# Odd layer's output product: two of four column chunks as a Strassen pair, streamed with the first chunk

## The chip, the cores and the metric

The kernel runs on one core of a Trainium2 chip. The metric is device time in microseconds of one execution. Before the change it is 1306.67 us, the median of three runs (1305.98 to 1306.85).

## The reference, cut to what matters

Two post-LayerNorm layers work on `x` of 256 tokens by 2048 channels, in fp32. The even layer is a Mamba-2 mixer beside block attention, with one output projection. The odd layer, where most of the change lies, is:

```python
u, gate = jnp.split(x @ w_in, 2, axis=-1)
y = jax.nn.gelu(s5_ssm(u, ...))
ga, gb = jnp.split(y @ w_glu, 2, axis=-1)
y = ga * jax.nn.sigmoid(gb)
h = (y * jax.nn.silu(gate)) @ w_out           # the odd layer's output product, 2048 x 2048
x = layer_norm(DEEPNORM_ALPHA * x + h, ln_g[layer], ln_b[layer])
```

## The kernel before, in words

**Weights.** Every weight matrix is read once from HBM, in units of 128 partitions by 1024 fp32 values (two K tiles of 128 rows by 512 output columns, 512 KB). A unit goes through three steps, all issued by `split_to` (L328): a load into a `raw` tile (four of them) on SyncE's queue (L361), a rounded copy `wh` on ScalarE (L367), and the remainder `wl = raw - wh` on VectorE (L372). The pool has four `wh`/`wl` pairs, and a unit is split three units ahead of its use. A product of activations and weights takes three matmuls per tile: high by high, high by low, low by high. `xmm` (L417) issues them with the activations as the stationary side: 128 tokens by 128 K rows against 512 columns. So a whole unit is 12 matmuls (two K tiles, two token halves, three terms).

**Strassen groups.** For the odd layer's GLU product, three pairs of column chunks (n1, n2) already use the scheme that the change extends (`product_fast`, L496, with the stream `STREAM`). Over eight of the 16 K tiles, seven products of quarter blocks take the place of eight. A unit of such a product is 6 matmuls (one token half). The names are: p1, q5, v2 and p4 use the weight block `a` (first as loaded, then after `b`, then `c`, then `d` were added to it in place), p3 and q7 use `c` (then `c + b`), and p2 uses `d`. n1 and n2 are the other eight K tiles, done in the plain way. A block is an SBUF tile `block`; "load" is a plain DMA, "add" a DMA issued by GpSimd that adds HBM data onto the block (L324), and "sum" an add on VectorE (L326). An add onto a block follows the split that read the block, and the next split of the block follows the add.

**Order around the change.** SyncE's queue carries the unit loads, in order; GpSimd's queue carries the adds, in order, and each of its DMAs waits in that queue for what it needs. Small work (residual adds, gates, transposes) is put into `jobs` and handed out by `pump` after each unit. A scheduler then fixes each engine's order.

**Output product before.** Four column chunks (j = 0 to 3) of eight units each follow one another: `first2` at L1855, j = 1 and 2 in the loop above `last`, each followed by a residual add and `bn_stats` (`res1`), and j = 3 in `product_apart` (L587), which does all eight units for the first token half and then for the second, so that LayerNorm of the first half runs beside the second. The eight split units of j = 3 are kept in a pool of their own (`tp2`).

**Rotary jobs.** In the even layer `rope_jobs` (L1126) queues two `rot` jobs, two empty ones and two `turn` jobs. `rot` ends with an add on GpSimd (L1143), and `turn` is four TensorE transposes (L626) of what it wrote.

Of the kernel before, what the change touches and what calls it, by code (L numbers as in the profile page):

```python
# [16 lines left out]
P = 128  # L17
# [20 lines left out]
def _stream():  # L38
    out, seen = [], {}
    for g in range(GROUPS):  # L40
        for s in FLOW if g else HEAD:
# [148 lines left out]
def trunk(tc, io, out):  # L190
# [4 lines left out]
    def nm(s):  # L195
        count[0] += 1
        return f"{s}_{count[0]}"

    with ExitStack() as top:
# [76 lines left out]
        for g in range(GROUPS):  # L276
            for k in range(2):
# [50 lines left out]
        def split_to(i):  # L328
            while nsplit[0] <= min(i, len(units) - 1):
                n = nsplit[0]  # L330
                for what in first.get(n, ()):
                    prepare(*what)
                if n in early:
                    with tc.issue_after(loaded[-1].ins):
                        early.pop(n)()
                if n in held_raw:
                    raw = blocks[held_raw[n]]
                elif n in room:
                    raw = keep[0].tile([P, UK, 512], F32R, tag=room[n], name=nm("raw")).bitcast(F32)
                else:  # L340
                    raw = st.tile([P, UK, 512], F32, tag="raw", name=nm("raw"))
                if n < 2:
                    wh = st.tile([P, UK, 512], F32R, tag="wh", name=nm("wh"))
                    wl = st.tile([P, UK, 512], F32R, tag="wl", name=nm("wl"))
                    for k in range(UK):
                        if k == 0:
                            xpart(n)
                        for lo, hi in ((0, 256), (256, 512)) if n + k == 0 else ((0, 512),):
                            loaded.append(nc.sync.dma_start(raw[:, k, lo:hi], units[n][:, k * 512 + lo : k * 512 + hi]))
                            with tc.issue_after(conv[-2].ins):  # L350
                                conv.append(A.activation(wh[:, k, lo:hi], raw[:, k, lo:hi], AF.Copy))
# [11 lines left out]
                wh = pool.tile([P, UK, 512], F32R, tag=th, name=nm("wh"))  # L363
# [4 lines left out]
                wl = pool.tile([P, UK, 512], F32R, tag=tl, name=nm("wl"))  # L368
                with ExitStack() as pin:
                    if hold[0] is not None:  # L370
                        pin.enter_context(tc.issue_after(hold[0]))
                    splits[n] = (loaded[-1], high, V.tensor_tensor(wl, raw, wh.bitcast(F32), op=OP.subtract))  # L372
                ready[n] = (wh, wl)
                for what in then.get(n, ()):
                    prepare(*what)
                nsplit[0] += 1
# [116 lines left out]
                    run(lambda o=o: total(o))  # L493
                then(h)

        def product_fast(stream, group, rest, turn):  # L496
# [6 lines left out]
            for i, (g, s, k) in enumerate(stream):  # L503
                if g not in made:
                    made[g] = group(g, lambda i, names=names: main.tile([P, 512], F32, tag=names[i], name=nm("main")))
                    names = [names[2], names[3], names[1], names[0]]
                split_to(unit[0] + 3)
                wh, wl = ready.pop(unit[0])
                ps, pieces, done = made[g][s]
                if s in ("n1", "n2"):  # L510
                    for j in range(UK):
                        for o in range(2):
                            xmm(ps, o, (wh, wl), j, rest(UK * k + j), s == "n2" and k + j == 0 and (o == 1 or (g, "z") not in open_), False, True)
# [138 lines left out]
        with ExitStack() as l0:  # L652
# [473 lines left out]
            def rope_jobs(ps, dst):  # L1126
# [378 lines left out]

        ax.close()

        with ExitStack() as l1:
# [174 lines left out]
            def scanned():  # L1683
                scan.close()
                gpool.append(l1.enter_context(tc.tile_pool(name="gp", bufs=1)))
                for n in ("n1", "n2", "n4"):
                    ops[n] = gpool[-1].tile([P, 2, 4, P], F32R, name=n)

            at(36, scanned)
            sg1 = wk.tile([P, 2, D], F32, tag="sg1", bufs=1, name="sg1")  # L1690
# [129 lines left out]
            def group(g, bank):  # L1820
# [20 lines left out]
                def one():  # L1841
# [5 lines left out]
                return {"p1": (X, lambda: whole(range(0, 4), 0), [copy("p1", "p1", X)]), "q5": (Y, lambda: summed("n1"), [copy("z5", "gt", Y)]),  # L1847
                        "v2": (X, lambda: summed("n2"), [less(0)]), "q7": (X, lambda: summed("s3"), [less(1)]),
                        "p3": (Z, lambda: summed("n4"), []), "p2": (Y, lambda: whole(range(4, 8), 0), []),
                        "p4": (X, lambda: whole(range(4, 8), 1), []), "n1": ((Y, X), None, []), "n2": ((Z, R), None, []),  # L1850
                        "second": (last2, second), "one": one}

            product_pair(y5hl, between, glu_jobs, lambda: y_split(3))
            product_fast(STREAM, group, lambda k: y5hl(8 + k), 1)
            first2 = product("x", y2hl)  # L1855

        with ExitStack() as l2:
            tp = l2.enter_context(tc.tile_pool(name="tp2", bufs=1))
            keep[0], keep[1] = tp, range(unit[0] + 2 * CU, unit[0] + 3 * CU)
            gb1 = big("A", [P, 4, D])  # L1860
            endp = l2.enter_context(tc.tile_pool(name="endp", bufs=1, space=PSUM))
            sums = [endp.tile([P, 512], F32, name=f"sum{i}") for i in range(2)]
            flip = endp.tile([2, P], F32, name="flip")
            gbr = tp.tile([2, 2 * NEND], F32, name="gbr")
            pair = tp.tile([P, 2], F32, name="pair")
            rowp = tp.tile([2, P], F32, name="rowp")
# [5 lines left out]
            def res1(ps, j, t):  # L1872
                dst = x1[:, t, 512 * j : 512 * j + 512]
                V.scalar_tensor_tensor(dst, dst, ALPHA, ps[t], op0=OP.mult, op1=OP.add)
                V.bn_stats(st1[:, t, j, :], dst)
# [78 lines left out]
```

## Time and profile before

| | before |
|---|---|
| median of three runs | 1306.67 us |
| the profiled execution | 1306.54 us |
| its span (first to last instruction) | 1304.8 us |
| TensorE matmul busy | 1296.0 us (99%) |
| VectorE / ScalarE / GpSimd busy | 1031.8 / 738.1 / 349.2 us |
| DMA moved | 300.90 MB, mean 231 GB/s |

The profile is of one execution. It gives each instruction's start and length, the idle time of the engine before it and what ended that idle time; the chain of waits follows the end of the program back from step to step. Matmuls overlap in the pipeline: one is shown as 0.39 us long, while the next starts 0.23 us after it. The queue that carries GpSimd's DMAs is called q0 software_dynamic, SyncE's is in q1 hardware_dynamic.

### The profile page before, as it was taken

The page shows a single profiled execution, that of the slowest core. Times are in us where ns is not written, and L with a number is a line of the kernel's source. Part 1 is how long each engine was busy: PE and PEld are TensorE (multiplying, and loading weights), DVE is VectorE, ACT ScalarE, POOL GpSimd, SP SyncE. Part 2 cuts the span into 40 slices and gives each one's busy share as a digit, 9 for nine tenths or more (in the row PEclk, how much of TensorE's full clock was granted, in tenths as well). Part 3 has the DMA queues.
Part 4 walks back from the last instruction along what each step waited for, and adds up shares of the span by engine and source line. Part 5 has one row for each costly group of instructions (what it writes and reads, how often), then busy time and mean ns, then how long its engine had stood idle before and what let it go on. Part 6 is the DMA issues. An engine that isn't in the chain of part 4 may idle for free.

```text
span 1304.8 us, 21605 instructions
## 1 busy us (share of the span) xinstructions
PE 1296.0 (99%) x7939; PEld 1089.7 (84%) x7939; DVE 1031.8 (79%) x1694; ACT 738.1 (57%) x1000; POOL 349.2 (27%) x649
## 2 busy tenths in 40 slices
PE   9999999999999999999999999999999999999997
PEld 9988888878888888888888888888888888888885
DVE  6778977885788888888877777858989859988665
ACT  6566668865644554464475555354355557666441
POOL 0044000125035767876820110022232001110000
PEclk9999999999999999999999999999999999999999
DMA  8555566565557766767768978469999789888762
GB/s 316 177 179 188 180 209 198 190 204 178 182 197 244 233 224 228 239 210 245 235 207 291 302 186 291 170 219 324 317 292 327 245 311 241 217 249 230 257 212 80
DMA packets 100094, 300.90 MB, mean 231 GB/s; under 512 B 19378, under 2 KB 29570, under 8 KB 99476
## 3 DMA queue, kind: packets, MB, share of 16 engines
q1 hardware_dynamic: 74356, 239.81, 55.0%
q0 software_dynamic: 11232, 46.18, 13.5%
q10 hardware_dynamic: 14400, 13.54, 3.2%
q8 instruction: 62, 1.02, 0.3%
q14 instruction: 44, 0.36, 0.1%
HBM read 276.93 MB, written 21.00 MB: 228 GB/s over the span
## 4 chain that ended last, share of the span: by engine, by line
PE 95%; POOL 2%; DVE 1%; DMA 1%; issue 0%; ACT 0%; SPq 0%; POOLq 0%
PE main L422 51%; PE main L478 17%; PE main L479 9%; PE main L521 7%; PE main L445 3%; PE aux L626 2%; POOL c L906 1%; PE aux L1084 1%; PE enc L1593 1%; PE dec L1638 1%; PE aux L982 1%; PE aux L1170 0%; DMA wb<-c 0%; POOL c L909 0%; DMA raw<-in_wi 0%; PE dec L1634 0%
## 5 line engine op out<-in xcount | busy, mean ns | idle before, releaser
L372 DVE TENSOR_TENSOR wl<-raw,wh 128x1024 fp32r<-128x1024 f32 x400 | 497.0, 1247 | 194.6 <-ACT wh L367 191.8
L367 ACT ACTIVATE wh<-raw 128x1024 fp32r<-128x1024 f32 x400 | 421.9, 1059 | 403.1 <-PE main L422 184.0
L422 PE MATMUL main<-wh,A 128*128 128x512 f32 x1216 | 392.5, 394 | 0.0
L478 PE MATMUL main<-A,wh 128*128 128x512 f32 x768 | 273.3, 400 | 0.0
L422 PEld LDWEIGHTS main<-wh,A 128*128 128x128 f32 x1216 | 227.9, 188 | 47.3 <-issue 0.7
L422 PE MATMUL main<-wh,C 128*128 128x512 f32 x832 | 265.1, 393 | 0.0
L422 PE MATMUL main<-wl,A 128*128 128x512 f32 x608 | 238.5, 392 | 0.0
L479 PE MATMUL main<-A,wl 128*128 128x256 f32 x768 | 215.5, 281 | 0.0
L422 PEld LDWEIGHTS main<-wh,C 128*128 128x128 f32 x832 | 155.9, 188 | 33.2
L478 PEld LDWEIGHTS main<-A,wh 128*128 128x128 f32 x768 | 144.2, 188 | 35.0 <-ACT b L1057 0.4
L422 PE MATMUL main<-wl,C 128*128 128x512 f32 x416 | 162.6, 391 | 0.0
L479 PEld LDWEIGHTS main<-A,wl 128*128 128x128 f32 x768 | 145.0, 189 | 0.4 <-issue 0.2
L422 PEld LDWEIGHTS main<-wl,A 128*128 128x128 f32 x608 | 114.3, 188 | 22.8 <-issue 0.2
L906 POOL TENSOR_TENSOR c<-c 128x8 f32<-128x8 f32 (+2 forms) x192 | 102.1, 550 | 27.8 <-DMA wb<-c 20.1
L422 PEld LDWEIGHTS main<-wl,C 128*128 128x128 f32 x416 | 78.1, 188 | 16.0
L372 DVE TENSOR_TENSOR wl<-block,wh 128x1024 fp32r<-128x1024 f32 x60 | 72.9, 1221 | 15.1 <-ACT wh L367 14.9
L367 ACT ACTIVATE wh<-block 128x1024 fp32r<-128x1024 f32 x60 | 63.1, 1060 | 36.5 <-PE main L422 20.1
L478 PE MATMUL main<-C,wh 128*128 128x512 f32 x192 | 68.3, 400 | 0.0
L1092 POOL TENSOR_TENSOR ssq<-ssq,c 128x256 f32<-128x256 f32 x16 | 18.0, 1128 | 161.1 <-ACT c L1090 160.4
L479 PE MATMUL main<-C,wl 128*128 128x256 f32 x192 | 53.5, 281 | 0.0
L908 POOL TENSOR_TENSOR c<-c,c 128x4 f32<-128x4 f32 (+2 forms) x96 | 42.2, 440 | 7.5
L324 POOL DMA_DIRECT2D block<-in_wglu x18 | 15.5, 916 | 104.0 <-DVE wl L372 86.7
(367 smaller groups left out, 1731.2 us busy)
## 6 DMA issues: line engine op xcount, KB each, us to landing
raw<-in_wi SPq DMA_DIRECT2D x270, 512.0 KB
raw<-in_wo SPq DMA_DIRECT2D x84, 512.0 KB
raw<-in_wglu SPq DMA_DIRECT2D x46, 512.0 KB
wt<-wb POOLq DMA_DIRECT2D x16, 896.0 KB, 8.3
block<-in_wglu POOLq DMA_DIRECT2D x20, 512.0 KB, 8.1
wb<-ob ACTq DMA_DIRECT2D x16, 512.0 KB
block<-in_wo POOLq DMA_DIRECT2D x12, 512.0 KB, 7.5
block<-in_wglu SPq DMA_DIRECT2D x12, 512.0 KB
```

Source lines behind the costliest of these rows:

```text
L324: added.append(nc.gpsimd.dma_start(blocks[g, name, k].rearrange("p k n -> p (k n)"), source[by][k], accum_op=OP.add))
L367: high = A.activation(wh, raw, AF.Copy)
L372: splits[n] = (loaded[-1], high, V.tensor_tensor(wl, raw, wh.bitcast(F32), op=OP.subtract))
L422: end = T.matmul(ps[o], l[:, k, sl], r[:, j, :], start=start and i == 0, stop=stop and i == 2, skip_group_check=free)
L445: T.matmul(pv[o // 2][:, o % 2, :], l[:, j, sl], r[:, k, :], start=first and i == 0 and o % 2 == 0, stop=end and i == 2 and o % 2 == 1, sk ...
L478: T.matmul(ps[o], wh[:, j, sl], xx[:, k, :, :].rearrange("p a n -> p (a n)"), start=first, stop=False, skip_group_check=True)
L479: lastmm[:] = [T.matmul(ps[o][:, S : 2 * S], wl[:, j, sl], xh[:, k, :], start=False, stop=end, skip_group_check=True)]
L521: lastmm[:] = [T.matmul(ps, p, q[:, j, :], start=begin, stop=False, skip_group_check=True)]
L626: end = T.transpose(dst[:, i * P : i * P + P], s, ident)
L906: G.tensor_tensor(p[:, :, :, 0:m], cs[:, :, :, 1 : m + 1], cs[:, i, :, n : n + 1].unsqueeze(1).to_broadcast([P, 2, 4, m]), op=OP.mult)
L908: G.tensor_tensor(cs[:, 0, :, n + 1 : n + 1 + m], p0[:, 0, :, 0:m], p1[:, 1, :, 0:m], op=OP.subtract)
L1092: G.tensor_tensor(ssq, ssq, jk[:, f, :], op=OP.add)
```

## The change

The first three column chunks of the output product become one stream (`LSTREAM`, handed to `product_fast`): chunk n0 plain, with its eight units, and chunks n1 and n2 as a Strassen pair over K tiles 0 to 7 (p and q names) and plain over tiles 8 to 15. That is 30 units, 16 of 12 matmuls and 14 of 6, in place of 24 units of 12. All weight sums of this pair are DMA adds. The left operands are sums of quarter blocks of `y2`, the product's input, kept as a high and a low part: `rows_job` copies two quarter pairs of the high part into two `block` tiles and adds the low part, all by GpSimd's DMAs; `pair_job` makes four sums of them on VectorE; `again` splits each into high and low on ScalarE and VectorE. These jobs are queued inside the last GLU group (`ahead`). The last chunk keeps four of its split units in the big tile `A`, the other four stay in the ordinary pool, and `LEAP` splits further ahead over the last six units of the stream. The pools of the end are replaced by tiles that exist already (`sg1`, `ut`, `gt` and two PSUM tiles), and the LayerNorm rows are loaded into `sg1`'s place. Rotary jobs get a third empty job.

```diff
+LAST = ("n0 n0 n0 p1 n0 p1 n0 n0 n0 n0 q5 q5 p3 n2 p3 n2 v2 v2 n2 n2 q7 q7 p2 n1 p2 n1 p4 p4 n1 n1").split()
+LSTREAM = [("f", s, LAST[:i].count(s)) for i, s in enumerate(LAST)]
+LEAP = [0] * (len(LAST) - 6) + [1, 1, 2, 2, 3, 4]
...
-        units += [io["wo1"][i] for i in range(io["wo1"].shape[0])]
+        n0, n1, n2, n3 = ([io["wo1"][CU * c + u] for u in range(CU)] for c in range(4))
+        sources["f"] = {"a": n1[0:2], "b": n2[0:2], "c": n2[2:4], "d": n1[2:4], "n0": n0, "n1": n1[4:], "n2": n2[4:]}
...
+        for k in range(2):
+            hook(first, "f", k, "p1", k - 4, "load", "a", "a")
+            hook(first, "f", k, "p1", 1 + k, "load", "c", "c")
+            at_item(then, "f", k, ("p1", k), "add", "a", "b")
+            at_item(then, "f", k, ("q5", k), "add", "a", "c")
+            at_item(then, "f", k, ("p3", k), "add", "c", "b")
+            at_item(then, "f", k, ("v2", k), "add", "a", "d")
+        units += n3
...
-                split_to(unit[0] + 3)
+                split_to(unit[0] + 3 + (leap[i] if leap else 0))
...
-                jobs.extend([rot(0), rot(1), rest, rest, turn(0), turn(1)])
+                jobs.extend([rot(0), rot(1), rest, rest, rest, turn(0), turn(1)])
...
-                return {"p1": (X, lambda: whole(range(0, 4), 0), [copy("p1", "p1", X)]), "q5": (Y, lambda: summed("n1"), [copy("z5", "gt", Y)]),
-                        "v2": (X, lambda: summed("n2"), [less(0)]), "q7": (X, lambda: summed("s3"), [less(1)]),
+                ahead = g == GROUPS - 1
+                return {"p1": (X, lambda: whole(range(0, 4), 0), [copy("p1", "p1", X)]),
+                        "q5": (Y, lambda: summed("n1"), [copy("z5", "gt", Y)] + [rows_job] * ahead),
+                        "v2": (X, lambda: summed("n2"), [less(0)] + [lambda: jobs.extend([pair_job(p) for p in FIRST])] * ahead),
+                        "q7": (X, lambda: summed("s3"), [less(1)] + [lambda: jobs.extend([again(p) for p in ("n1", "n2", "n4", "s3")])] * ahead),
...
+            def rows_job():
+                for i in range(2):
+                    whole2[i] = gpool[-1].tile([P, UK, 512], F32, tag="block", bufs=8, name=nm("block")).rearrange("p k (f n) -> p (k f) n", n=S)
+                for i in range(2):
+                    nc.gpsimd.dma_start(whole2[i], y2["h"][:, 4 * i : 4 * i + 4, :].bitcast(F32))
+                for i in range(2):
+                    nc.gpsimd.dma_start(whole2[i], y2["l"][:, 4 * i : 4 * i + 4, :].bitcast(F32), accum_op=OP.add)
...
             product_fast(STREAM, group, lambda k: y5hl(8 + k), 1)
-            first2 = product("x", y2hl)
...
+            keep[0], keep[1] = keeper, range(unit[0] + len(LAST), unit[0] + len(LAST) + 4)
+            product_fast(LSTREAM, outer1, lambda i: y2hl(8 + i), 0, LEAP)
...
-            for j in range(3):
-                ps = product("x", y2hl, prelude=lambda u: split_to(unit[0] + 3 + u) if j == 2 else None) if j else first2
-                for t in range(2):
-                    jobs.append(lambda ps=ps, j=j, t=t: res1(ps, j, t))
```

`outer1` (new) is the stream's counterpart of `group`: p1, v2, q7 and p4 accumulate in one PSUM bank, q5 and p2 in a second, p3 with n2 and n1 in further ones, and VectorE adds or subtracts each into the residual `x1`, 9 passes over 128 by 512 for chunks n1 and n2 where there were 4.

How the change moves instructions on GpSimd's queue, in the last two GLU groups: the blocks 11667 and 11681 belong to the group before the last, 12015 and 12029 are the last group's `a`, 12117 and 12133 its `c`. Before:

```order
L324 DMA block_11667<-in_wglu 128x1024 [waits DMASW7_49,DMASW3_49,DVE_49]
L324 DMA block_11681<-in_wglu 128x1024 [waits DMASW4_49,DMASW0_49,DVE_49]
L324 DMA block_12015<-in_wglu 128x1024 [waits DMAHW1_49,DMASW5_49,DVE_49]
L324 DMA block_12029<-in_wglu 128x1024 [waits DMAHW3_49,DMASW6_49,DVE_49]
L324 DMA block_12117<-in_wglu 128x1024 [waits DMAHW5_49,DVE_49]
L324 DMA block_12133<-in_wglu 128x1024 [waits DMAHW7_49,DVE_49]
```

and after (12238 and 12239 are the two tiles of `rows_job`, `C_11454` is `y2`):

```order
L343 DMA block_11667<-in_wglu 128x1024 [waits DMASW7_49,DMASW3_49,DVE_49]
L343 DMA block_11681<-in_wglu 128x1024 [waits DMASW4_49,DMASW0_49,DVE_49]
L1885 DMA block_12238<-C_11454 128x4x256 [waits DMASW5_49,DMASW1_49,DVE_49]
L1885 DMA block_12239<-C_11454 128x4x256 [waits DMASW6_49,DMASW2_49,DVE_49]
L1887 DMA block_12238<-C_11454 128x4x256 [waits DMASW5_49]
L1887 DMA block_12239<-C_11454 128x4x256 [waits DMASW6_49]
L343 DMA block_12015<-in_wglu 128x1024 [waits DMAHW1_49,DVE_49]
L343 DMA block_12029<-in_wglu 128x1024 [waits DMAHW3_49,DVE_49]
L343 DMA block_12117<-in_wglu 128x1024 [waits DMAHW5_49,DMASW3_49,DVE_49]
L343 DMA block_12133<-in_wglu 128x1024 [waits DMAHW7_49,DMASW4_49,DVE_49]
```

The four DMAs of `rows_job` stand ahead of the last group's first adds, and the second two of them wait in the queue for the first two to land.

On TensorE in the even layer, at one of the rotary turns (`b_549` and `b_556` are what the two `rot` jobs wrote). Before:

```order
L422 MATMUL main_3867<-wh_3903,A_73 128x512
L626 MATMUL aux_4048<-consts,b_549_3886 128x128 x4
L422 MATMUL main_3866<-wh_3961,A_73 128x512
L422 MATMUL main_3866<-wl_3963,A_73 128x512
...
L422 MATMUL main_3867<-wh_3961,A_73 128x512
L626 MATMUL aux_4084<-consts,b_556_3919 128x128 x4
```

and after:

```order
L442 MATMUL main_3867<-wh_3903,A_73 128x512
L442 MATMUL main_3866<-wh_3961,A_73 128x512
L442 MATMUL main_3866<-wl_3963,A_73 128x512
...
L442 MATMUL main_3867<-wl_3963,A_73 128x512
L442 MATMUL main_3867<-wh_3961,A_73 128x512
L646 MATMUL aux_4078<-consts,b_549_3886 128x128 x4
```

The turn stands one unit of 12 matmuls later.

## Rows read from the trace of the kernel before

**Rows 1.** The profile page: its first line.
```profile
span 1304.8 us, 21605 instructions
```

**Rows 2.** Chain of waits from 1130 us: start us, us, what.
```profile
1159.28 2.77 PE main L521 x12
1162.05 5.44 PE main L422 x24
1167.49 2.72 PE main L521 x12
...
1170.44 1.36 PE main L521 x6
1171.80 2.49 PE main L422 x11
...
1215.59 79.11 PE main L422 x346
```

**Rows 3.** Timeline of TensorE, 512 to 522 us: start, length, instruction, idle before.
```profile
517.88 0.66 PE L626 MATMUL aux<-consts,b 128*128 128x128 f32 x4 [0.96 <-POOL b L1143]
```

**Rows 4.** Busy time by stretch: PE, PEld, DVE, ACT, POOL, clock, DMA share, GB/s.
```profile
1164.00:1172.00 8.00, 8.00 (x37) 6.64 (x36) 7.84 (x10) 5.54 (x9) 0.86 (x1) 1.00 0.43 105
1181.00:1206.00 25.00, 25.00 (x114) 20.69 (x113) 20.51 (x22) 15.41 (x18) 0.00 (x0) 1.00 0.74 227
1206.50:1294.70 88.20, 88.20 (x390) 72.47 (x389) 53.41 (x61) 35.69 (x38) 3.78 (x4) 1.00 0.57 192
```

**Rows 5.** Timeline of GpSimd, 1133 to 1156 us: the adds onto blocks.
```profile
1133.61 0.86 POOL L324 DMA_DIRECT2D block<-in_wglu  x1 [2.08 <-DVE wl L372]
1135.18 0.86 POOL L324 DMA_DIRECT2D block<-in_wglu  x1 [0.71 <-DVE wl L372]
1153.25 0.86 POOL L324 DMA_DIRECT2D block<-in_wglu  x1 [17.20 <-DMA raw<-in_wglu]
1154.98 0.86 POOL L324 DMA_DIRECT2D block<-in_wglu  x1 [0.87 <-DVE wl L372]
```

**Rows 6.** DMA view, one stretch per add of Rows 5: us to landing at the end.
```profile
block<-in_wglu POOLq DMA_DIRECT2D x1, 512.0 KB, 10.3
...
block<-in_wglu POOLq DMA_DIRECT2D x1, 512.0 KB, 12.5
...
block<-in_wglu POOLq DMA_DIRECT2D x1, 512.0 KB, 5.4
...
block<-in_wglu POOLq DMA_DIRECT2D x1, 512.0 KB, 6.4
```

**Rows 7.** DMA queues, 1148.5-1153 and 1156-1159 us: packets, MB, engines' share.
```profile
q1 hardware_dynamic: 517, 1.87, 102.1%
...
q0 software_dynamic: 158, 0.58, 103.7%
```

**Rows 8.** Timeline of SyncE: first and last of six loads issued from 1136.8 us.
```profile
1136.88 0.45 SPq L319 DMA_DIRECT2D block<-in_wglu  x1
...
1150.64 0.33 SPq L361 DMA_DIRECT2D raw<-in_wglu  x1
```

**Rows 9.** Timelines of VectorE and ScalarE in the same stretch.
```profile
1141.55 1.23 DVE L372 TENSOR_TENSOR wl<-block,wh 128x1024 fp32r<-128x1024 f32 x1
...
1162.03 2.38 DVE L372 TENSOR_TENSOR wl<-block,wh 128x1024 fp32r<-128x1024 f32 x2
...
1167.13 1.22 DVE L372 TENSOR_TENSOR wl<-block,wh 128x1024 fp32r<-128x1024 f32 x1
...
1160.94 2.21 ACT L367 ACTIVATE wh<-block 128x1024 fp32r<-128x1024 f32 x2 [0.41 <-PE main L521]
```

**Rows 10.** VectorE by line, 1206.5 to 1294.7 us: count, busy, mean ns, idle before.
```profile
L372 DVE TENSOR_TENSOR wl<-raw,wh 128x1024 fp32r<-128x1024 f32 x29 | 35.3, 1224 | 24.7 <-ACT wh L367 24.7
L1874 DVE SCALAR_TENSOR_TENSOR D<-D,main 128x512 f32<-128x512 f32 x7 | 4.8, 680 | 5.1 <-PE main L422 5.1
```

More of the change, by code (lines that the diff above doesn't have):

```diff
@@ L290, in trunk @@
                 hook(then, g, k, "v2", k, "add", "a", "d")
-        units += [io["wo1"][i] for i in range(io["wo1"].shape[0])]
+        n0, n1, n2, n3 = ([io["wo1"][CU * c + u] for u in range(CU)] for c in range(4))
+        sources["f"] = {"a": n1[0:2], "b": n2[0:2], "c": n2[2:4], "d": n1[2:4], "n0": n0, "n1": n1[4:], "n2": n2[4:]}
+        for g, s, k in LSTREAM:
+            place[g, s, k] = len(units)
+            if s in ("n0", "n1", "n2", "p2"):
+                units.append(sources[g]["d" if s == "p2" else s][k])
+            else:
+                held_raw[len(units)] = (g, "c" if s in ("q7", "p3") else "a", k)
+                units.append(None)
+        for k in range(2):
[6 more added lines that the diff above has]
+        units += n3
         ready = {}
@@ L362, in split_to @@
                 pool, th, tl = (keep[0], f"wh{n % 8}", f"wl{n % 8}") if n in keep[1] else (st, "wh", "wl")
-                wh = pool.tile([P, UK, 512], F32R, tag=th, name=nm("wh"))
+                own = n in keep[1] and callable(keep[0])
+                wh = keep[0](n, 0) if own else pool.tile([P, UK, 512], F32R, tag=th, name=nm("wh"))
                 with ExitStack() as pin:
@@ L367, in split_to @@
                     high = A.activation(wh, raw, AF.Copy)
-                wl = pool.tile([P, UK, 512], F32R, tag=tl, name=nm("wl"))
+                wl = keep[0](n, 1) if own else pool.tile([P, UK, 512], F32R, tag=tl, name=nm("wl"))
                 with ExitStack() as pin:
@@ L494, in product_wide, with product_fast @@
                 then(h)
-        def product_fast(stream, group, rest, turn):
+        def product_fast(stream, group, rest, turn, leap=None):
             names = [f"m{(turnno[0] - turn + i // 2) % 2}{i % 2}" for i in range(4)]
@@ L506, in product_fast @@
                     names = [names[2], names[3], names[1], names[0]]
-                split_to(unit[0] + 3)
+                split_to(unit[0] + 3 + (leap[i] if leap else 0))
                 wh, wl = ready.pop(unit[0])
-                ps, pieces, done = made[g][s]
-                if s in ("n1", "n2"):
+                ps, pieces, done = made[g][s]() if callable(made[g][s]) else made[g][s]
+                if s in ("n0", "n1", "n2"):
                     for j in range(UK):
                         for o in range(2):
-                            xmm(ps, o, (wh, wl), j, rest(UK * k + j), s == "n2" and k + j == 0 and (o == 1 or (g, "z") not in open_), False, True)
+                            xmm(ps, o, (wh, wl), j, (pieces or rest)(UK * k + j), k + j == 0 and (s == "n0" or s == "n2" and (o == 1 or (g, "z") not in open_)), False, True)
                     if s == "n2":
@@ L1506, in trunk @@
         ax.close()
-        with ExitStack() as l1:
+        l1 = enter(ExitStack())
+        if True:
             wk = l1.enter_context(tc.tile_pool(name="wk1", bufs=2))
@@ L1686, in scanned @@
                 for n in ("n1", "n2", "n4"):
-                    ops[n] = gpool[-1].tile([P, 2, 4, P], F32R, name=n)
+                    ops[n] = gpool[-1].tile([P, 2, 4, P], F32R, tag=n, bufs=1, name=nm(n))
             at(36, scanned)
@@ L1851, in group @@
                         "second": (last2, second), "one": one}
+            FIRST = (("n1", (0, 1), (1, 1), OP.subtract), ("n2", "n1", (0, 0), OP.subtract),
+                     ("n4", "n2", (1, 0), OP.add), ("s3", (0, 0), (0, 1), OP.subtract))
+            whole2, sums2, ops2 = {}, {}, {}
+            def rows_job():
[5 more added lines that the diff above has]
+                    nc.gpsimd.dma_start(whole2[i], y2["l"][:, 4 * i : 4 * i + 4, :].bitcast(F32), accum_op=OP.add)
@@ new lines, in pair_job, with go, again @@
+            def pair_job(what):
+                def go():
+                    name, x, y, op = what
+                    i = len(sums2)
+                    sums2[name] = sg1[:, i // 2, 512 + 512 * (i % 2) : 1024 + 512 * (i % 2)].rearrange("p (f n) -> p f n", f=4)
+                    x, y = (sums2[v] if isinstance(v, str) else whole2[v[0]][:, :, v[1] * P : v[1] * P + P] for v in (x, y))
+                    V.tensor_tensor(sums2[name], x, y, op=op)
+                return go
+            def again(name):
+                def go():
+                    if name == "s3":
+                        t = w1("ut", [P, 2, 4, P], 1, F32R)
+                    else:
+                        t = gpool[-1].tile([P, 2, 4, P], F32R, tag=name, bufs=1, name=nm(name))
+                    ops2[name] = t
+                    A.activation(t[:, 0], sums2[name], AF.Copy)
+                    V.tensor_tensor(t[:, 1], sums2[name], t[:, 0].bitcast(F32), op=OP.subtract)
+                return go
@@ L1853, in trunk, with part1 @@
             product_pair(y5hl, between, glu_jobs, lambda: y_split(3))
             product_fast(STREAM, group, lambda k: y5hl(8 + k), 1)
-            first2 = product("x", y2hl)
[L1857 to L1866, printed above, removed]
+            def part1(j, t):
+                return x1[:, t, 512 * j : 512 * j + 512]
@@ new lines, in stat1, with more1, scale1, res1 @@
+            def stat1(j, t):
+                V.bn_stats(st1[:, t, j, :], part1(j, t))
+            def more1(j, t, ps):
+                return lambda: V.tensor_tensor(part1(j, t), part1(j, t), ps, op=OP.add)
+            def scale1(j, t, ps):
+                return lambda: V.scalar_tensor_tensor(part1(j, t), part1(j, t), ALPHA, ps, op0=OP.mult, op1=OP.add)
+            def res1(ps, j, t):
+                scale1(j, t, ps[t])()
+                stat1(j, t)
+            def outer1(g, bank):
+                X, Y = bank(0), bank(1)
+                ps0 = [bank(2), bank(3)]
+                zr = []
+                def ZR():
+                    if not zr:
+                        zr.extend([bank(2), bank(3)])
+                    return zr
+                def less1(t):
+                    return lambda: V.tensor_tensor(part1(2, t), part1(2, t), X, op=OP.subtract)
+                def piece(k, t):
+                    return lambda: [(y2["h"][:, i, t * P : t * P + P], y2["l"][:, i, t * P : t * P + P]) for i in range(4 * k, 4 * k + 4)]
+                def summed2(name):
+                    return lambda: [(ops2[name][:, 0, i, :], ops2[name][:, 1, i, :]) for i in range(4)]
+                def second():
+                    for t, ps in enumerate(ZR()):
+                        jobs.extend([more1(2, t, ps), lambda t=t: stat1(2, t)])
+                def one():
+                    more1(1, 0, Y)()
+                    scale1(1, 1, X)()
+                    jobs.extend([lambda t=t: stat1(1, t) for t in range(2)])
+                return {"n0": (ps0, y2hl, [lambda: jobs.extend([lambda t=t: res1(ps0, 0, t) for t in range(2)])]),
+                        "p1": (X, piece(0, 0), [scale1(1, 0, X)]), "q5": (Y, summed2("n1"), [scale1(2, t, Y) for t in range(2)]),
+                        "v2": (X, summed2("n2"), [less1(0)]), "q7": (X, summed2("s3"), [less1(1)]),
+                        "p3": lambda: (ZR()[0], summed2("n4"), []), "p2": (Y, piece(1, 0), []), "p4": (X, piece(1, 1), []),
+                        "n1": ((Y, X), None, []), "n2": lambda: (ZR(), None, []), "second": (last_of(LSTREAM, g), second), "one": one}
@@ new lines, in trunk, with keeper @@
+            half = big("A", [P, 4, D], F32R)
+            def keeper(n, low):
+                i = n - keep[1].start
+                return half[:, i, 1024 * low : 1024 * low + 1024].rearrange("p (k n) -> p k n", k=UK)
+            keep[0], keep[1] = keeper, range(unit[0] + len(LAST), unit[0] + len(LAST) + 4)
+            product_fast(LSTREAM, outer1, lambda i: y2hl(8 + i), 0, LEAP)
+            gb1 = wk.tile([P, 2, D], F32, tag="sg1", bufs=1, name="gb1")
+            both = sp.tile([P, 2, 512], F32, tag="enc", name=nm("sums"))
@@ L1867, in trunk @@
+            sums = [both[:, i, :] for i in range(2)]
+            flip = sp.tile([P, 2, 512], F32, tag="dec", name=nm("flip"))[0:2, 0, 0:P]
+            gbr = w1("ut", [P, 4, S], 1).rearrange("p a b -> p (a b)")[0:2, 0 : 2 * NEND]
+            small = w1("gt", [P, 2, 256])
+            pair, rowp = small[:, 0, 0:2], small[0:2, 1, 0:P]
             nc.sync.dma_start(gbr, io["lnr"][2:4, 0 : 2 * NEND])
@@ L1870, in trunk @@
             nc.gpsimd.dma_start(gb1[:, 1, :], lnrow(3))
[L1872 to L1875, printed above, removed]
-            for j in range(3):
-                ps = product("x", y2hl, prelude=lambda u: split_to(unit[0] + 3 + u) if j == 2 else None) if j else first2
-                for t in range(2):
-                    jobs.append(lambda ps=ps, j=j, t=t: res1(ps, j, t))
             def last(ps):
```

## The prediction

> **What bounds the kernel now.** I read the busy shares first, then the chain of waits, the lines, the waits of single engines, and the DMA view. TensorE is busy 1296.0 us of the 1304.8 us span [rows 1], and the last product alone is one unbroken piece of the chain, 346 matmuls in 79.11 us [rows 2]. That is 79.11 / 346 = 0.2286 us from one matmul to the next. So here a matmul left out is time saved, if the next one is ready; every unit that comes late is time lost. What must be read is therefore: how many matmuls go, and whether the weight splits (ScalarE, VectorE) and the adds onto blocks (GpSimd's queue) still come in time.
>
> **Matmuls.** Before, the output product has 4 x 8 units of 12 matmuls, 384. After, the stream has 16 units of 12 and 14 of 6, 276, and the last chunk 96: 372. Twelve fewer at 0.2286 us are -2.74 us. This is small because the Strassen pair covers half of the K tiles and saves one product of eight over them.
>
> **Rotary turn.** One TensorE instruction of the even layer waits 0.96 us for the add on GpSimd [rows 3]. With the turn one unit (12 x 0.2286 = 2.74 us) later in the same stream, the add is done by then. What is late next is nothing I can see: the transposes feed work that is some units away. I take -1.0 us; bounds 0 (if the next transposes wait instead) and -1.1.
>
> **Work beside the last product.** Six more unit splits (30 + 8 against 32), each 1.22 us on VectorE and about 1.05 on ScalarE, and five more passes over 128 by 512 at 0.68 us [rows 10]: 6 x 1.22 + 5 x 0.68 = 10.7 us on VectorE, which has 88.2 - 53.4 = 34.8 us free there, with DMA at 0.57 of its time [rows 4]. TensorE hides it on the average. In the Strassen part a unit lasts only 6 x 0.2286 = 1.37 us and its split 1.22, so there VectorE falls behind; but plain units of 2.74 us stand between. The adds of this part have no queue ahead of them but the two LayerNorm rows of 1 MB. I cost it at 0, bounds 0 and +2 (the first units of the last chunk may come late, since a split is no longer kept for all eight).
>
> **The end of the GLU product.** Four pair sums, and four low parts of the split sums, are eight VectorE operations over 128 by 512, about 0.68 us each: 5.5 us. In 1181 to 1206 us VectorE is busy 20.51 of 25 us [rows 4], so 4.5 us are free: about 1 us too much, which the three units of split lead can absorb. I cost it at 0, bounds 0 and +1.
>
> **The four DMAs of `rows_job`.** These are what I forecast to cost. They stand in GpSimd's queue ahead of the last group's adds `a += b`. The trace of before shows that queue so:
>
> - The two adds before are issued at 1133.61 and 1135.18 us and land after 10.3 and 12.5 us, at 1143.9 and 1147.7 [rows 5, 6]. The second lands 3.8 us after the first, though issued 1.6 after it: the adds go one after another, and one takes 3.8 us beside SyncE's loads.
> - By the queues' bytes, a load of 512 KB with the engines to itself takes 4.5 us x 0.524 / 1.87 = 1.26 us, and an add 3 us x 0.524 / 0.58 = 2.7 us [rows 7]. Together 3.96, near the 3.8: in shared times one add and one load pass in turn.
> - The last group's adds are issued at 1153.25 and 1154.98 and land after 5.4 and 6.4 us, at 1158.7 and 1161.4 [rows 5, 6].
>
> After, the two copies can be issued when the split at 1141.55 us has ended (1142.8) [rows 9], run from 1147.7, and each shares with a load: 2 x 1.26 = 2.5 us, to 1150.2 and 1152.7. The two accumulates, at 3.8, end at 1156.5 and 1160.3, and the adds `a += b` then at 1164.1 and 1167.9 in place of 1158.7 and 1161.4. No row of before shows a DMA from SBUF to SBUF or with pieces of 1 KB (256 fp32 values). The bounds I use are the rows' own: an accumulate between 1.26 us (a load) and 6.5 us (3.8 + 2.7), nearest row 3.8, which I take, since it too is a DMA that adds 512 KB onto a block.
>
> Who waits: the second `a += b` is read by the split of q5. Before, its second `wl` begins at 1162.03 + 1.2 = 1163.2, and behind it on VectorE stand a sum, a turn, a sum, and p3's `wl`, which ends at 1167.13 + 1.22 = 1168.35 [rows 9]: 5.15 us. With `wh` at 1.1, p3 is ready 6.25 us after the landing. TensorE begins p3 at 1170.44 [rows 2], so a landing up to 1164.2 costs nothing. A landing at 1167.9 makes p3 ready at 1174.15: 3.7 us late. Part of this delay falls earlier: six loads are issued from 1136.88 to 1150.64 [rows 8], and if one passes with each of GpSimd's transfers, the fourth and fifth (n1) land at about 1160.3 and 1164.1. With 1.1 + 1.23 us for a split they are ready at 1162.65 and 1166.45, where TensorE begins them at 1162.05 and 1164.77 [rows 2]: 0.6 us and then 1.1 us more, both inside the 3.7. The unit behind p3 is split after it on a VectorE that is busy 7.84 of 8 us there [rows 4], so nothing is made up; I add 0.6 for it. Cost +4.3. Bounds: with 1.26 us for each accumulate the landing comes at 1162.8, below 1164.2: 0. With 6.5, each of the two 2.7 later: 4.3 + 5.4 = +9.7.
>
> **Sum.** 1306.54 (the profiled execution, 1304.8 its span) - 2.74 - 1.0 + 4.3 = 1307.1 us. The median of three is 0.13 us above the profiled execution, so 1307.2 against 1306.67. Differences within 0.2% (2.6 us: 1304.05 to 1309.3) are about what a measurement can't tell from no change.
>
> **Rivals.**
>
> *A, the DMAs hide.* If the four DMAs move like plain loads, 4 x 1.26 = 5.0 us, they fit between 1147.7 and 1153.25, in which the queue was empty. For it: that gap, and the six loads were issued well ahead of their use. Against it: in 1148.5 to 1153 the loads held the engines at 102% [rows 7], and an add measured 2.7 alone. Then 1306.67 - 2.74 - 1.0 = 1302.9 us. The Trainium skill ("DMA: Bandwidth & Descriptors", section "Anatomy of one DMA — SWDGE (gpsimd) path") puts every DMA of this path at 2.0 us plus its bytes at 436 GB/s, 1.2 us for 512 KB by my estimate, without a higher price for adds. The trace agrees for the plain load (1.26) and not for the add (2.7).
>
> *B, slower: the accumulates from 1 KB pieces.* If reading the pieces and adding makes an accumulate over 1.1 us longer than the 3.8 (two of them 2.2 us, which with 0.5 us passes the bound of 0.2%), the forecast turns into slower: at 6.5 each, 1307.2 + 5.4 = 1312.6 us. For it: no row shows these pieces cheap, and the second pair waits for the first to land. Against it: bytes and partitions are those of the adds seen. The same page, in "Why small descriptors are slow (HBM only)", says that transfers between SBUF and SBUF don't suffer from small pieces, which would speak for A; no run so far shows one.
>
> *C, the last chunk comes late.* The last product's early units wait for their splits after the stream's short units, +1 to +2 us on the forecast: 1308.2 to 1309.2 us.
>
> *D, the turn only moves its wait* (0 in place of -1.0): 1308.2 us. It needs GpSimd's add to be over 2.74 us later than it is; the wait was 0.96.
>
> **How the numbers follow.** The forecast, with between 1.3 and 6 us of the DMAs' cost showing, 0.40; A 0.32; B 0.18; C 0.08; D 0.02. Faster takes A and no more: 0.32. Slower takes B, a part of C and the upper end of the forecast (a cost over 6.4 us in all): 0.25. The same: 0.43. The likeliest case alone reaches from 1304.2 to 1309. The range has to take in A, at 1302.9 and a little under it, and most of B: 1302.6 to 1311.5; above it stays the last part of B, up to 1312.6 and 1314 with C.
>
> **What would show it.** The landing of the last group's two adds `a += b`, from issue, against 5.4 and 6.4 us: the forecast has them at about 1164 and 1168 on the old clock (1 us less after the turn's gain). TensorE idle for some 4 us from n1 to p3 of the last GLU group, released by `wh`/`wl` of VectorE or ScalarE. The wait of the rotary transposes gone. The last product one piece of the chain, without waits. The forecast is wrong if TensorE stays busy in the last GLU group (A), if accumulates land over 5 us apart (B), or if TensorE waits inside the last product (C).

## The result: 0.74% slower, and the profile after

The changed kernel takes 1315.93 us, the median of six runs (1314.35 to 1317.69), against 1306.51 us for the kernel before on the same chip: a ratio of 1.0074, 95% interval 1.0063 to 1.0084. The forecast was 1307.2 us, no change, with a range up to 1311.5; the time lies above the range. In the profiled execution the span grew by 9.4 us, against [rows 1]:

```profile
span 1314.2 us, 21626 instructions
```

**Where TensorE lost it.** The timeline of TensorE after, 1160 to 1190 us (start, length, instruction, and in brackets the idle time before it and what ended it), has four waits where the kernel before has none [rows 2]:

```profile
1170.87 0.50 PE L541 MATMUL main<-wh,n 128*128 128x512 f32 x1 [2.20 <-ACT wh L387]
1172.12 0.80 PE L541 MATMUL main<-wl,n 128*128 128x512 f32 x1 [0.76 <-DVE wl L392]
...
1175.96 0.79 PE L541 MATMUL main<-wl,n 128*128 128x512 f32 x1 [0.46 <-DVE wl L392]
...
1180.51 0.80 PE L541 MATMUL main<-wh,n 128*128 128x512 f32 x1 [1.62 <-DVE p L1863]
```

The first wait begins at 1170.87 - 2.20 = 1168.67 us. Before, the same unit (q5 of the last GLU group) began at 1167.49 [rows 2], so 1.18 us had been lost by then, all of it in the even layer (below). The last wait is p3's. The matmul that ends it lasts 0.80 us, where the one that ended the first wait, still at the full clock, lasted 0.50. The busy time by stretch of the kernel after (PE, PEld, DVE, ACT, POOL, granted clock, DMA share, GB/s) has it at 0.50, the lower of its two levels (1.2 GHz), from about 1171 to 1185 us, after TensorE had stood still for 2.2 us; before, it was 1.00 throughout this stretch [rows 4]:

```profile
1168.00:1171.00 3.00, 0.80 (x4) 0.34 (x3) 0.16 (x1) 1.06 (x1) 0.00 (x0) 1.00 1.03 284
1171.00:1174.00 3.00, 2.24 (x5) 1.54 (x6) 1.07 (x1) 0.41 (x1) 0.00 (x0) 0.56 0.46 172
1174.00:1177.00 3.00, 2.46 (x6) 1.14 (x5) 2.32 (x3) 3.00 (x5) 0.00 (x0) 0.50 0.00 0
...
1180.00:1183.00 3.00, 2.49 (x6) 2.01 (x7) 3.00 (x5) 1.85 (x3) 0.85 (x1) 0.50 0.44 44
...
1186.00:1189.00 3.00, 3.00 (x17) 2.49 (x16) 1.43 (x2) 1.64 (x2) 0.85 (x1) 1.00 1.05 209
```

**What it waited for.** The chain of waits of the kernel after (start, length, what) names it piece by piece:

```profile
1142.37 8.68 DMA block<-C
1151.06 0.84 issue
1151.90 1.30 POOL block L1887
...
1154.98 1.14 POOL block L343
1156.11 17.38 DMA block<-in_wglu
...
1173.60 1.06 ACT wh L387
...
1177.59 1.13 DVE block L345
1178.72 1.13 DVE wl L392
1179.86 0.61 DVE p L1863
...
1180.51 2.93 PE main L541 x6
1183.44 3.33 PE main L442 x11
```

A copy of `rows_job` lands, its add can be issued, behind it the second `a += b` of the last GLU group, and that takes 17.38 us to land, where it took 6.4 [rows 6]. Then come `wh`, `wl`, the sums, p3's `wl`, a pass over p3's bank, and p3 on TensorE. The decisive row is one of GpSimd's timeline, an idle time of 7.00 us at the third line here:

```profile
1142.37 0.79 POOL L1885 DMA_DIRECT2D block<-C  x1 [5.15 <-DVE wl L392]
1144.12 0.78 POOL L1885 DMA_DIRECT2D block<-C  x1 [0.96 <-DVE wl L392]
1151.90 1.30 POOL L1887 DMA_DIRECT2D block<-C  x1 [7.00 <-DMA block<-C]
1154.21 1.28 POOL L1887 DMA_DIRECT2D block<-C  x1 [1.01 <-DMA block<-C]
1154.98 2.34 POOL L343 DMA_DIRECT2D block<-in_wglu  x2
```

The DMA view gives the time from issue to landing (the last figure) of the two copies, the two adds and the first `a += b`:

```profile
block<-C POOLq DMA_DIRECT2D x1, 512.0 KB, 8.7
block<-C POOLq DMA_DIRECT2D x1, 512.0 KB, 9.8
block<-C POOLq DMA_DIRECT2D x1, 512.0 KB, 10.2
block<-C POOLq DMA_DIRECT2D x1, 512.0 KB, 11.7
block<-in_wglu POOLq DMA_DIRECT2D x1, 512.0 KB, 14.7
```

So the copies land at 1151.1 and 1153.9, the adds at 1162.1 and 1165.9, the first `a += b` at 1154.98 + 14.7 = 1169.7 and the second at 1156.11 + 17.38 = 1173.5, against 1158.7 and 1161.4 before [rows 5, 6]. From the second copy's landing to the first add's it is 8.2 us, while the landings on either side of this gap are 2.9 and 3.8 us apart. In a part of the gap GpSimd's queue moves nothing and SyncE's loads have the DMA engines to themselves. The queues after, 1154.9 to 1156 us (packets, MB, share; no packet of q0), show it:

```profile
q1 hardware_dynamic: 127, 0.45, 103.7%
```

**The account,** by the starts of the chain's pieces. q5: 1168.67 against 1167.49, +1.18 (the even layer). p3: 1180.51 against 1170.44 [rows 2], +10.07, so 8.89 from the landing. The two pieces behind it take 2.93 + 3.33 us where they took 1.36 + 2.49 [rows 2]: 2.41 more, nearly all of it the clock, and TensorE is 12.48 us late. The last matmul ends at 1303.88 against 1215.59 + 79.11 = 1294.70 [rows 2], +9.18: the last product gives 3.30 back.

### The profile page after: what moved, and what is told of

The parts are those of the page before. It is cut to its first block, busy times and chain, and to the rows that moved or that the text cites. A ratio compares the mean times of both kernels' runs of the same rounds, so it can differ in the third digit from the quotient of the medians.

```text
span 1314.2 us, 21626 instructions
## 1 busy us (share of the span) xinstructions
PE 1299.9 (99%) x7927; PEld 1090.3 (83%) x7927; DVE 1047.3 (80%) x1713; ACT 745.1 (57%) x1010; POOL 356.8 (27%) x661
## 4 chain that ended last, share of the span: by engine, by line
PE 88%; issue 5%; DVE 3%; DMA 3%; POOL 1%; ACT 1%; SPq 0%; POOLq 0%; DVEq 0%; ACTq 0%
PE main L442 46%; PE main L498 17%; PE main L499 9%; PE main L541 5%; PE main L465 3%; PE aux L646 2%; DMA block<-in_wglu 1%; DVE wl L392 1%; POOL block L343 1%; PE aux L1104 1%; DMA block<-C 1%; DMA raw<-in_wi 1%; PE aux L1002 1%; PE enc L1614 1%; PE dec L1659 1%
## 5 line engine op out<-in xcount | busy, mean ns | idle before, releaser
L387 ACT ACTIVATE wh<-raw 128x1024 fp32r<-128x1024 f32 x390 | 411.4, 1059 | 393.4 <-PE main L442 181.9
L392 DVE TENSOR_TENSOR wl<-raw,wh 128x1024 fp32r<-128x1024 f32 x390 | 485.7, 1250 | 176.0 <-ACT wh L387 171.7
L442 PE MATMUL main<-wh,C 128*128 128x512 f32 x736 | 237.2, 393 | 0.0
L442 PEld LDWEIGHTS main<-wh,C 128*128 128x128 f32 x736 | 138.0, 188 | 29.1
L442 PE MATMUL main<-wl,C 128*128 128x512 f32 x368 | 143.8, 391 | 0.0
L392 DVE TENSOR_TENSOR wl<-block,wh 128x1024 fp32r<-128x1024 f32 x72 | 87.5, 1220 | 29.3 <-ACT wh L387 29.1
L387 ACT ACTIVATE wh<-block 128x1024 fp32r<-128x1024 f32 x72 | 75.7, 1059 | 54.3 <-PE main L442 24.0
L442 PEld LDWEIGHTS main<-wl,C 128*128 128x128 f32 x368 | 69.1, 188 | 13.9
L343 POOL DMA_DIRECT2D block<-in_wo x20 | 17.3, 865 | 158.4 <-DVE wl L392 89.4
```

Source lines behind the costliest of these rows:

```text
L343: added.append(nc.gpsimd.dma_start(blocks[g, name, k].rearrange("p k n -> p (k n)"), source[by][k], accum_op=OP.add))
L442: end = T.matmul(ps[o], l[:, k, sl], r[:, j, :], start=start and i == 0, stop=stop and i == 2, skip_group_check=free)
```

## The experiments

Seven kernels were run, each against the kernel before on its own chip.

**1. Two empty jobs again.** (e1_after_two_empty) The changed kernel with the old rotation:

```diff
-                jobs.extend([rot(0), rot(1), rest, rest, rest, turn(0), turn(1)])
+                jobs.extend([rot(0), rot(1), rest, rest, turn(0), turn(1)])
```

> The changed kernel with two empty jobs in the rotation, as before the change. Theory R: in the trace after, TensorE is 1.1 us later than before by the end of the even layer (0.9 us of it lost by 325 us, 1.2 won at the turn, 1.4 lost again by 593 us), so the third empty job costs about 1 us net: 1314.9 us, against 1315.9. Rival, the prediction's own step: the third empty job gains 1.0 us, and the loss in the even layer comes from something else: 1316.9 us.

Measured: 1314.45 us, before 1305.86 on that chip; ratio 1.0063 (1.0050 to 1.0075). That is 8.6 us over before, where the changed kernel is 9.4 over it: 0.8 less, in the direction of theory R, but within the intervals.

**2. The third empty job alone,** (e2_before_three_empty) in the kernel before (the same edit the other way round).

> The kernel before with the third empty job alone. Theory R: about 1 us slower, 1307.5 us, with the wait of 0.96 us at the turn gone and the same small losses near 305 and 563 us as in the trace after. Rival, the prediction's own step: 1.0 us faster, 1305.5 us.

Measured: 1306.62 against 1305.86 us, ratio 1.0003 (0.9995 to 1.0012). The gain of 1.0 us of the prediction's step (a ratio of 0.9992) is outside the interval; a loss of 1 us is inside it. The groups of TensorE by line, 300 to 311 us (count, busy, mean ns, idle before), show what the job costs. In experiment 1, with two empty jobs:

```profile
L1104 PE MATMUL aux<-b,C 128*64 128x256 f32 x8 | 1.3, 392 | 0.0
L1102 PE MATMUL aux<-b,C 128*64 128x128 f32 x8 | 0.8, 272 | 0.0
```

and in experiment 2, with three:

```profile
L1084 PE MATMUL aux<-b,C 128*64 128x256 f32 x8 | 1.9, 392 | 0.0
L1082 PE MATMUL aux<-b,C 128*64 128x128 f32 x8 | 1.4, 279 | 0.0
```

The same sixteen short matmuls are busy 1.2 us more in all, at the same mean length: they overlap less where the later turn puts them. All five traces with three empty jobs show 1.9 and 1.4, all four with two show 1.3 and 0.8. And the wait of 0.96 us that the job was to remove [rows 3] is there in three of the four traces with two empty jobs (0.9 to 1.0 us), and in none with three. By the starts of the same matmuls in two traces, experiment 2 against before, TensorE falls 0.85 us back at these sixteen and wins 1.2 at the turn, and nothing more changes up to 596 us: the two effects nearly cancel. The trace after also has three new waits at the turns, 0.7 us in all, which experiment 2 has not.

**3. The second pair without the adding:** (e3_rows_no_add)

```diff
-                    nc.gpsimd.dma_start(whole2[i], y2["l"][:, 4 * i : 4 * i + 4, :].bitcast(F32), accum_op=OP.add)
+                    nc.gpsimd.dma_start(whole2[i], y2["l"][:, 4 * i : 4 * i + 4, :].bitcast(F32))
```

> The second pair of rows_job's DMAs as plain copies in place of adds (leaves out the high part of four sums). Their place in the queue and their wait for the first pair stay. Theory Q, the wait in the queue: the first add a += b is late because the second pair is issued only when the first has landed, and then needs some 10 us from issue to landing; without the adding the second pair lands about 1.3 us sooner each, 2.6 us in all, so the last a += b lands at about 1171 us in place of 1173.5, and the time falls by 2.6 to 4 us (what the lower clock adds included): 1312 to 1313.3 us. Rival B of the prediction, the adding from small pieces is the price: the delay goes almost wholly with it, 1304 to 1308 us.

Measured: 1311.05 against 1305.86 us, ratio 1.0036 (1.0024 to 1.0048): 5.2 us over before where the changed kernel is 9.4 over it, so 4.2 us are gone, a little more than theory Q's 4, and far from the 8 to 12 of rival B. The timeline of GpSimd in this run still has the wait, 7.45 us, and the last `a += b` still lands over 13 us after its issue:

```profile
1143.95 0.78 POOL L1885 DMA_DIRECT2D block<-C  x1 [0.96 <-DVE wl L392]
1152.18 0.75 POOL L1887 DMA_DIRECT2D block<-C  x1 [7.45 <-DMA block<-C]
```

The cheap second pair lands 7.7 and 8.0 us after its issue, where the adds took 10.2 and 11.7. So some seven tenths of the time of such a pair is there without the adding. The landings of this run's second and third copy, from issue, separate the dependence from the adding:

```profile
block<-C POOLq DMA_DIRECT2D x1, 512.0 KB, 10.1
block<-C POOLq DMA_DIRECT2D x1, 512.0 KB, 7.7
```

They are at 1143.95 + 10.1 = 1154.05 and 1152.18 + 7.7 = 1159.9, 5.8 us apart, and the copies on either side of this gap land 2.7 and 2.5 us apart. So some 3.1 us go with the wait alone, among DMAs of one kind. The last `a += b` lands at 1169.3, 4.2 us earlier than in the changed kernel, where theory Q had 2.6; whether the 1.6 between them are the price of adding from 1 KB pieces, no run separates. The granted clock fell here too (0.50 from 1178 to 1181 us).

**4. The adds behind the last `c += b`:** (e4_adds_behind)

```diff
-                for i in range(2):
-                    nc.gpsimd.dma_start(whole2[i], y2["l"][:, 4 * i : 4 * i + 4, :].bitcast(F32), accum_op=OP.add)
+                with tc.issue_after(added[-1].ins):
+                    for i in range(2):
+                        nc.gpsimd.dma_start(whole2[i], y2["l"][:, 4 * i : 4 * i + 4, :].bitcast(F32), accum_op=OP.add)
```

> The copies of rows_job stay where they are, and its two adds are put behind the last group's c += b, so that nothing waits behind them but a += d. Theory Q: a += b is issued at about 1153 and 1155 us and lands near 1160 and 1163.5, the waits of TensorE at 1168 to 1181 us go, and its clock stays at 1.00: 11.3 us less, 1304.6 us. Rival, the bytes: four DMAs of 512 KB on engines that are at 100 per cent delay the loads and adds wherever they stand, and some 4 us of the loss remain: 1308 us or more.

Measured: 1310.22 against 1305.86 us, ratio 1.0031 (1.0019 to 1.0044). That is 5.1 us less than the changed kernel, not 11.3; by its total the run speaks for the rival, by its trace for Q. The wait at q5 is gone and p3 waits 1.21 us, the granted clock stays at 1.00 there, but a loss comes back later. The timelines of TensorE and then VectorE in this run:

```profile
1172.08 0.50 PE L541 MATMUL main<-wh,n 128*128 128x512 f32 x1 [1.21 <-DVE p L1863]
...
1193.62 0.50 PE L541 MATMUL main<-wl,ut 128*128 128x512 f32 x1 [3.05 <-DVE wl L392]
```

```profile
1191.13 0.69 DVE L1896 TENSOR_TENSOR sg<-block,block 128x512 f32<-128x512 f32 x1 [6.48 <-DMA block<-C]
...
1192.34 1.22 DVE L392 TENSOR_TENSOR wl<-block,wh 128x1024 fp32r<-128x1024 f32 x1
```

VectorE's first pair sum now waits 6.48 us for the adds of `rows_job`, and q7's split stands behind it. The two adds have no good place among the two tried: ahead of `a += b` they delay it, behind `c += b` they are late themselves. The chain of this run shows the landing of the second:

```profile
1176.56 14.48 DMA block<-C
```

It lands at 1191.0, and the first at 1175.8 + 10.2 = 1186.0: 5.0 us apart, here with loads beside them.

**5. No DMAs: the sums on VectorE.** (e5_sum_vector)

```diff
-                for i in range(2):
-                    nc.gpsimd.dma_start(whole2[i], y2["h"][:, 4 * i : 4 * i + 4, :].bitcast(F32))
-                for i in range(2):
-                    nc.gpsimd.dma_start(whole2[i], y2["l"][:, 4 * i : 4 * i + 4, :].bitcast(F32), accum_op=OP.add)
+                for i in range(2):
+                    V.tensor_tensor(whole2[i], y2["h"][:, 4 * i : 4 * i + 4, :].bitcast(F32), y2["l"][:, 4 * i : 4 * i + 4, :].bitcast(F32), op=OP.add)
```

> The four DMAs of rows_job are replaced by two adds on VectorE (high part plus low part, 128 by 1024), 1.22 us each; three empty jobs in the rotation. Theory Q: the last group's a += b is issued near 1153 and 1155 us with nothing ahead of it in the queue and lands as before the change (5.4 and 6.4 us after issue), TensorE doesn't wait between 1168 and 1181 us, and only the 12 matmuls fewer are left: 2.8 us below before, plus 0 to 1 us for the empty job: 1303.7 to 1304.7 us where before is 1306.5. Rival, VectorE is full: in 1181 to 1206 us 20.51 + 5.5 + 2.44 = 28.5 us of work stand against 25, TensorE waits some 3 us there: 1307 us or more.

Measured: 1304.08 against 1306.51 us, ratio 0.998 (0.9971 to 0.9989): faster than before, as theory Q had it, and 11.9 us below the changed kernel. TensorE has no wait between 1140 us and the end of the last product.

**6. The same, with two empty jobs.** (e6_sum_vector_two)

> As e5_sum_vector, with two empty jobs as before the change. Theory Q: 2.8 us below before, 1303.7 us where before is 1306.5, and 0 to 1 us below e5. Rival, VectorE is full: as e5, 1306.5 us or more. If the third empty job gains 1.0 us, as the prediction had it, this run is 1 us above e5.

Measured: 1303.26 against 1306.51 us, ratio 0.9973 (0.9964 to 0.9982). This version beats both kernels. GpSimd's timeline has the two `a += b` as the kernel before has them [rows 5], and they land 5.5 and 6.5 us after issue (5.4 and 6.4 before, [rows 6]); the sums are one row of VectorE's timeline:

```profile
1151.90 0.86 POOL L343 DMA_DIRECT2D block<-in_wglu  x1 [16.57 <-DVE wl L392]
1153.64 0.86 POOL L343 DMA_DIRECT2D block<-in_wglu  x1 [0.87 <-DVE wl L392]
```

```profile
1171.35 2.35 DVE L1885 TENSOR_TENSOR block<-C 128x1024 f32<-128x1024 f32 x2
```

The rival, a VectorE that is too full, is excluded: in the stretch of this run that about answers to 1181 to 1206 us of before [rows 4], VectorE is busy 24.37 of 25 us, and TensorE all of them at clock 1.00:

```profile
1179.00:1204.00 25.00, 25.00 (x112) 20.71 (x111) 24.37 (x29) 17.34 (x22) 0.26 (x1) 1.00 0.84 257
```

The third empty job comes out 0.8 us slower here too (5 against 6), the third comparison with that sign, none of them beyond its interval. Experiments 5 and 6 take away the dependence and the 2 MB of these DMAs together. No run kept the bytes in the queue without the dependence, so what the wait costs by itself is read from the traces of the changed kernel and experiment 3.

**7. The sums on GpSimd,** (e7_sum_gpsimd) with two empty jobs: `nc.gpsimd.tensor_tensor` in place of `V.tensor_tensor`, pinned behind the last group's `a += b`.

> As e6_sum_vector_two, but with the two adds on GpSimd, behind a += b in its queue. By GpSimd's 1.13 us for 128 by 256 an add over 128 by 1024 takes some 4.5 us, 9 us for both, from 1156 to 1165 us, where GpSimd has nothing to do until the first c += b near 1170. Theory Q: nothing waits, 1303.7 us where before is 1306.5, and not slower than e6. Rival: the adds take much longer or slow VectorE down beside them, and c += b is late: 1306 us or more.

Measured: 1309.83 against 1306.51 us, ratio 1.0027 (1.0016 to 1.0038). The rival is right in its second form: VectorE is slowed, while the adds are shorter than I had them. The timelines of GpSimd, VectorE and TensorE in this run show GpSimd's two adds in 5.02 us (2.5 each, not my 4.5), one split of VectorE that lasts 6.45 us in place of 1.22 in just this time, and TensorE waiting 3.67 us for it (the granted clock is 0.71 and 0.72 in the two stretches of 3 us from 1161 us):

```profile
1155.16 5.02 POOL L1886 TENSOR_TENSOR block<-C 128x1024 f32<-128x1024 f32 x2
```

```profile
1154.82 6.45 DVE L392 TENSOR_TENSOR wl<-block,wh 128x1024 fp32r<-128x1024 f32 x1
```

```profile
1161.33 0.50 PE L541 MATMUL main<-wl,A 128*128 128x512 f32 x1 [3.67 <-DVE wl L392]
```

## Why the prediction was wrong, step by step

**The step that failed** is "The two accumulates, at 3.8, end at 1156.5 and 1160.3". I let the four DMAs run back to back, each behind the one before. They did not: an add onto a copied tile must wait in the queue until the copy has landed, and is only then issued. The first add was issued at 1151.90 and needed 10.2 us to land, so it ended at 1162.1, 5.6 us after my number. Of these, 1.2 are the late start of the whole stretch (the second copy, too, lands at 1153.9 in place of 1152.7), and 4.4 are the gap: 8.2 us from one landing to the next where I had 3.8. The spacing from there on was as I had it (1162.1, 1165.9, 1169.7, 1173.5: 3.8 us each), and so was that of the copies (2.9 us, 2.5 forecast). The order of the queue, which stood in front of me with its waits, said that the adds wait for the copies; I wrote it into the order and did not give it a price.

Experiment 3 shows some 3.1 us of such a gap with plain copies. It also shows how much goes with the adding: 4.2 us of the time; what is left over before, 5.2 us, is still there without it. Why the first add needed 10.2 us from issue to landing, when an add on the emptier queue of before needed 5.4 [rows 6], stays in part open: SyncE's loads had the engines when it was issued, and no run took them away.

The Trainium skill ("DMA: Bandwidth & Descriptors", section "Anatomy of one DMA — SWDGE (gpsimd) path") says that a DMA engine never waits on a semaphore: a wait is done by the issuing sequencer, before the DMA is dispatched. The trace agrees (7.00 us of idle time on GpSimd, ended by the copy). This is the sentence that I should have weighed against the change.

**Rival B** was slower, on the right side, at 1312.6 us, but by another mechanism: small pieces that make an accumulate dear. As the whole price it is excluded by experiment 3, and its time came near by luck. In the changed kernel its sign did not show: the adds from 1 KB pieces landed 3.8 us apart. But that is no like for like with the 3.8 of [rows 6], since hardly a load passed beside them (0.01 MB from 1162 to 1164 us), and in experiment 4, where loads passed, they landed 5.0 us apart. So some price of the small pieces is likely, and not measured. Rival A failed as well: its 1.26 us is a load of SyncE's queue [rows 7], which says nothing of adds that wait.

**The chain behind the landing** was right but 0.7 us short: 3.7 as forecast, 4.4 and 0.7 make 8.8 of the 8.89. The 0.6 us for the unit behind p3 did not show. I had p3 ready 6.25 us after the landing; it began 7.0 us after it (1180.51 against 1173.5), because a pass over p3's bank (`p<-main`, L1863) stands behind its `wl` on VectorE, which I left out. Experiment 3 has the same 7.0 us between landing and p3 (1169.3 and 1176.3), and so has experiment 4 (1165.1 and 1172.1).

**The clock** was no term of my sum. After TensorE's waits, p3 and the first of the 11 matmuls behind it ran at the lower level, and these 17 cost 2.41 us more. In experiment 4, with single waits of 1.21 and 3.05 us, the granted clock was 0.999 over the run; in experiment 7 it fell behind a single wait of 3.67 us. These runs do not settle what brings the drop.

**The late loads** of n1, 0.6 and 1.1 us, did not show: TensorE's first wait is q5's. It made no difference to the sum, as they lay inside p3's delay.

**The turn,** -1.0 us, was +1.18 in the profile and is a loss of zero to one microsecond by the runs (experiments 1, 2, 5 and 6). The wait went, as forecast, so rival D did not happen. By the starts of the same matmuls, after against before, TensorE is 0.9 us back at 326 us (the sixteen short matmuls), 0.3 ahead at 540 (the wait is gone) and 1.1 back at 596. This last loss, of which three new waits are 0.7 us, comes with the third empty job in the changed kernel alone: 0.4 to 1.4 us in its four traces, none in experiment 2 and none with two empty jobs. Its cause stays open. No row of before could have shown these losses, but the reordering of TensorE's work around the turns could have warned me, and a bound of 0 for this step was too good.

**The matmuls,** -2.74 us, measured -3.30. The forecast twelve are there; the mean distance of two matmuls in the last product also fell, from 79.11 / 346 = 0.2286 us [rows 2] to 0.2269 in the longest unbroken piece of the chain after:

```profile
1279.83 24.05 PE main L442 x106
```

Over 372 matmuls that is 372 x 0.0017 = 0.6 us; why it fell, no run shows. Rival C did not happen: TensorE has no wait in the last product after, though VectorE is busier there (64.67 of 85.5 us, against 53.41 of 88.2 [rows 4]):

```profile
1218.40:1303.90 85.50, 85.50 (x382) 70.75 (x381) 64.67 (x76) 43.65 (x47) 10.64 (x12) 1.00 0.75 227
```

The eight small VectorE operations at the end of the GLU product and the two LayerNorm rows cost nothing, as forecast.

The miss of 8.7 us is thus the turn (1.18 in place of -1.0, so 2.2) and the DMAs (8.89 + 2.41 = 11.3 in place of 4.3, so 7.0: the gap 4.4, the clock 2.4, the chain 0.7, less the 0.6 that did not show), less 0.6 at the matmuls: 8.6.

## What to carry to other kernels

In an in-order queue, price a DMA that needs another DMA's result by the whole round trip, issue to landing, and not by its bytes: here one such dependence put a gap of 8.2 us between two landings where the forecast had 3.8, and all that was queued behind it came later by the difference. And before work is moved from an engine to a queue because the engine looks busy, look for what stands behind it there: two VectorE adds of 1.2 us, on an engine that was busy nearly all the time but had nobody waiting for it there, replaced four DMAs and turned a loss of 0.74% into a gain of 0.20% (experiment 5; 0.27% with the old rotation).

## What the runs showed of the hardware that was not expected

- **VectorE stood still beside elementwise work of GpSimd.** While GpSimd added two 128 by 1024 pairs (5.02 us), VectorE's subtraction of the same size took 6.45 us in place of 1.22. The Trainium skill ("SBUF — State Buffer", section "SBUF: two separate sides") says that the two share a port pair which one instruction holds as a whole while the other stands still, when VectorE reads two SBUF inputs and GpSimd's instruction reads SBUF; the trace agrees, and it held for both of GpSimd's instructions in a row. Which came first the trace leaves open: by it VectorE's began at 1154.82 and GpSimd's at 1155.16, though VectorE's was the one held, and times on GpSimd are rough.
- **A waiting TensorE can pay twice.** Waits of 2.20, 0.76, 0.46 and 1.62 us went with a granted clock of 0.50 for about 14 us, and 17 matmuls on the path took 2.41 us more. Waits of 1.21 and 3.05 us in experiment 4 did not.
- **A DMA from SBUF to SBUF in 1 KB pieces** is not cheaper than a load from HBM: the copies landed 2.7 to 2.9 us apart beside SyncE's loads (the changed kernel, experiments 3 and 4), where a load and a copy at a load's price would take 2.5.
